# The first large load issued from ScalarE, beside the short first load from SyncE

## The chip, the cores and the metric

One core of one Trainium2 chip, nothing else running on it. The time is that of one execution in device microseconds; a lower number is better.

## The reference

```python
x = np.random.randn(32, 256, 4096).astype(np.float32)
result = np.zeros((32, 256, 256), dtype=np.float32)
for i in range(256):
    result[:, :, i] = np.max(x[:, :, 16 * i : 16 * (i + 1)], axis=-1)
```

Max pooling over windows of 16 floats (64 B): 134 MB are read, 8.4 MB written, and each input is compared once.

## The kernel before

The kernel streams windows through a ring of two slots in SBUF. Each slot has room for 1024 windows and a gap of 152 more (GAP). A load alternates between the start of its slot and a place 152 windows further on. VectorE reduces each load in two parts: first the 872 windows that the next load of this slot will overwrite, then the 152 others. So the next load of a slot waits for the long part only. A short first load (FIRST) uses the gap of slot 0, and its maxima go into `kept` like the others.

```python
CHUNK, GAP, FIRST = 1024, 152, 132
LOADS_A, LOADS_B = 9, 6
last = total - FIRST - (LOADS_A + LOADS_B) * CHUNK          # 892
ring = pool.tile([P, 2 * (CHUNK + GAP) * W], fp32, ...)     # W = 16
# ... pooled(dst, at, n): reduce_max of n windows of the ring on VectorE
for g, loads in enumerate(([FIRST] + [CHUNK] * LOADS_A, [CHUNK] * LOADS_B + [last])):
    ...
    for n in loads:
        if n == FIRST:
            nc.sync.dma_start(out=ring[:, CHUNK * W : (CHUNK + n) * W], in_=xn)
            pooled(dst, CHUNK, n)
        else:
            low = n_loads % 2 * (CHUNK + GAP)
            moved = n_loads // 2 % 2
            at = low + moved * GAP
            nc.sync.dma_start(out=ring[:, at * W : (at + n) * W], in_=xn)
            if n == CHUNK:
                cut = CHUNK - GAP if moved else GAP
                parts = [(0, cut), (cut, n)]
                for u, v in parts if moved else parts[::-1]:
                    pooled(dst[:, u:v], at + u, v - u)
            ...                                             # the last load
            n_loads += 1
# ... one store from ScalarE, two from SyncE
```

In this text S is the short load, L0, L1, L2 are the large ones in order. L0 and L1 fill the two slots at once; L2 goes to slot 0 again and is the first that has to wait. It overwrites S's bytes too.

Of the kernel before, what the change touches and what calls it, by code (L numbers as in the profile page):

```python
# [1 line left out]

# [4 lines left out]


@with_exitstack
def kernel(  # L10
    ctx: ExitStack,
    tc: tile.TileContext,
    x: bass.AP,
    output_size: bass.AP,
    out: bass.AP,
):








    nc = tc.nc
    P = nc.NUM_PARTITIONS
    fp32 = mybir.dt.float32

    B, C, L = x.shape
    O = int(output_size)  # L30
    assert L % O == 0, (L, O)
    W = L // O
    total = B * C * O // P
    assert B * C * O % P == 0

    CHUNK = 1024
    GAP = 152
    FIRST = 132
    LOADS_A, LOADS_B = 9, 6
    last = total - FIRST - (LOADS_A + LOADS_B) * CHUNK  # L40
    assert 0 < last and last * (W + 1) <= CHUNK * W

    pool = ctx.enter_context(tc.tile_pool(name="pool", bufs=1))
    ring = pool.tile([P, 2 * (CHUNK + GAP) * W], fp32, tag="ring", name="ring")
    kept = pool.tile([P, total - last], fp32, tag="kept", name="kept")

    xw = x.flatten_outer_dims().rearrange("r (o w) -> (r o) w", w=W)
    ow = out.flatten_outer_dims().rearrange("r o -> (r o)")

    def pooled(dst, at, n):  # L50

        nc.vector.reduce_max(  # L52
            out=dst,
            in_=ring[:, at * W : (at + n) * W].rearrange("p (n w) -> p n w", w=W),
            axis=mybir.AxisListType.X,
        )

    taken = 0

    def group(n):  # L60

        nonlocal taken
        span = slice(taken * P, (taken + n) * P)
        taken += n
        return (
            xw[span].rearrange("(p n) w -> p (n w)", p=P),
            ow[span].rearrange("(p n) -> p n", p=P),
        )

    stores = []  # L70
    n_loads = 0
    base = 0
    for g, loads in enumerate(
        ([FIRST] + [CHUNK] * LOADS_A, [CHUNK] * LOADS_B + [last])
    ):
        xg, og = group(sum(loads))
        a = 0
        for n in loads:
            xn = xg[:, a * W : (a + n) * W]
            dst = kept[:, base + a : base + a + n] if n != last else None  # L80
            if n == FIRST:

                nc.sync.dma_start(  # L83
                    out=ring[:, CHUNK * W : (CHUNK + n) * W], in_=xn
                )
                pooled(dst, CHUNK, n)
            else:

                low = n_loads % 2 * (CHUNK + GAP)
                moved = n_loads // 2 % 2  # L90
                at = low + moved * GAP
                nc.sync.dma_start(out=ring[:, at * W : (at + n) * W], in_=xn)
                if n == CHUNK:
                    cut = CHUNK - GAP if moved else GAP
                    parts = [(0, cut), (cut, n)]
                    for u, v in parts if moved else parts[::-1]:
                        pooled(dst[:, u:v], at + u, v - u)
                else:
                    end = (at + CHUNK) * W
                    last_kept = ring[:, end - n : end]  # L100
                    pooled(last_kept, at, n)
                n_loads += 1
            a += n
        full = a - last if g else a
        stores.append((og[:, 0:full], kept[:, base : base + full]))
        base += full
    assert taken == total

    nc.scalar.dma_start(out=og[:, full : full + last], in_=last_kept)
    tc.no_sync_barrier()  # L110
    for dst, src in stores:
        nc.sync.dma_start(out=dst, in_=src)


# [1 line left out]
_INS = ['x', 'output_size']  # L116
_OUTS = [((32, 256, 256), 'float32')]

_NUMBERS = {'output_size': 256}


# [26 lines left out]
```

## Time and profile before

| | before |
|---|---|
| time, median | 335.11 us (334.94 to 335.2, 3 runs) |
| span of the profiled execution | 333.4 us |
| VectorE busy | 276.5 us (83%) |
| DMA packets, share of 16 engines | 98.7% + 0.3% |
| L0 lands, L2 issued, L2 lands | 25.14, 39.88, 63.85 us |

### The profile page before, as it was taken

To read this page: it belongs to the slowest core of one execution; us is meant where nothing else is said; L and a number is where in the kernel's file an instruction comes from. 1 tells how busy PE (TensorE), PEld (TensorE's weight loads), DVE (VectorE), ACT (ScalarE), POOL (GpSimd) and SP (SyncE) were. 2 spreads that over 40 slices of the span, in tenths; PEclk is the share of its full clock that TensorE was granted. 3 is DMA by queue.
4 is the path that set the end of the run, shared out by engine and by line. 5 is a ranking of instruction groups with operands and counts; after the bars stand their busy time and mean duration, and the time that the engine had idled before them with its cause. 6 is when DMAs were issued, how large, how long until landed. Compare 5 with 4: busy or idle time off the path is not lost.

```text
span 333.4 us, 113 instructions
## 1 busy us (share of the span) xinstructions
DVE 276.5 (83%) x32; POOL 0.2 (0%) x4
## 2 busy tenths in 40 slices
DVE  2009979797997979799797979979797997979993
POOL 0000000000000000000000000000000000000000
DMA  9898989999898989999898989999898989899997
GB/s 381 377 503 377 495 385 480 401 401 480 377 503 377 503 377 480 401 393 488 377 503 377 503 377 480 401 425 456 377 503 377 503 377 495 385 455 438 397 402 317
DMA packets 2880, 142.61 MB, mean 428 GB/s; under 512 B 320, under 2 KB 320, under 8 KB 448
## 3 DMA queue, kind: packets, MB, share of 16 engines
q1 hardware_dynamic: 2736, 142.15, 98.7%
q10 hardware_dynamic: 144, 0.46, 0.3%
HBM read 134.22 MB, written 8.39 MB: 428 GB/s over the span
## 4 chain that ended last, share of the span: by engine, by line
DMA 58%; DVE 36%; DVEq 5%; issue 0%; SPq 0%
DMA ring<-in_x_dram 58%; DVE kept L52 36%; DVEq L143 5%; SPq L83 0%
## 5 line engine op out<-in xcount | busy, mean ns | idle before, releaser
L52 DVE TENSOR_REDUCE kept<-ring 128x872 f32<-128x13952 f32 (+2 forms) x31 | 261.5, 8477 | 51.8 <-DMA ring<-in_x_dram 51.8
L52 DVE TENSOR_REDUCE ring<-ring 128x892 f32<-128x14272 f32 x1 | 15.0, 15009 | 0.0
L129 POOL MEMSET const-bfloat16-1.0<- 128x1 bf16 x1 | 0.1, 102 | 0.0
L129 POOL MEMSET const-uint8-127<- 128x1 uint8 x1 | 0.1, 102 | 0.0
L129 POOL MEMSET const-float32-1.0<- 128x1 f32 x1 | 0.1, 99 | 0.0
L129 POOL MEMSET const-float32-0.0<- 128x1 f32 x1 | 0.1, 98 | 0.2 <-issue 0.2
## 6 DMA issues: line engine op xcount, KB each, us to landing
ring<-in_x_dram SPq DMA_DIRECT2D x1, 7136.0 KB, 21.5
out_dram<-kept SPq DMA_DIRECT2D x1, 4674.0 KB, 32.2
out_dram<-kept SPq DMA_DIRECT2D x1, 3072.0 KB, 18.0
ring<-in_x_dram SPq DMA_DIRECT2D x1, 1056.0 KB, 5.1
out_dram<-ring ACTq DMA_DIRECT2D x1, 446.0 KB, 4.2
ring<-in_x_dram SPq DMA_DIRECT2D x15, 24.0
```

The lines of the kernel that those rows point to most:

```text
L52: nc.vector.reduce_max(out=dst, in_=ring[:, at * W : (at + n) * W].rearrange("p (n w) -> p n w", w=W), axis=mybir.AxisListType.X,)
L129: nc = _bacc.Bacc("TRN2", target_bir_lowering=False, num_devices=1)
L143: with _tile.TileContext(nc) as tc:
```

## The change

The intent is to start both first loads at once: S from SyncE, L0 from ScalarE. S becomes 128 windows (rows of 8 KB), one load of the first group 1020, and the last 900.

```diff
-    FIRST = 132
+    FIRST = 128
     LOADS_A, LOADS_B = 9, 6
-    last = total - FIRST - (LOADS_A + LOADS_B) * CHUNK
+    LESS = 4
+    group_a = [FIRST] + [CHUNK] * (LOADS_A - 1) + [CHUNK - LESS]
+    last = total - sum(group_a) - LOADS_B * CHUNK
+    group_b = [CHUNK] * LOADS_B + [last]
 ...
-                nc.sync.dma_start(out=ring[:, at * W : (at + n) * W], in_=xn)
-                if n == CHUNK:
+                queue = nc.scalar if n_loads == 0 else nc.sync
+                queue.dma_start(out=ring[:, at * W : (at + n) * W], in_=xn)
+                if n != last:
```

More of the change, by code (lines that the diff above doesn't have):

```diff
@@ L72 @@
     base = 0
-    for g, loads in enumerate(
-        ([FIRST] + [CHUNK] * LOADS_A, [CHUNK] * LOADS_B + [last])
-    ):
+    for g, loads in enumerate((group_a, group_b)):
         xg, og = group(sum(loads))
```

## The prediction

> **What bounds the kernel now.** I began with the page: busy shares by engine, and under them the moved bytes of each DMA queue.
>
> ```profile
> DVE 276.5 (83%) x32; POOL 0.2 (0%) x4
> ...
> q1 hardware_dynamic: 2736, 142.15, 98.7%
> q10 hardware_dynamic: 144, 0.46, 0.3%
> ```
>
> VectorE is busy for 83% of 333.4 us, but the packets of the SyncE queue (q1) fill 98.7% of what 16 DMA engines can give. The ScalarE queue (q10) carries only the last store. So the kernel is a DMA stream: 134.22 MB of loads and 8.39 MB of stores. The second view, busy time and DMA share by stretch, shows that the stream has no holes in the middle, only at its two ends (columns: stretch, length, VectorE busy, GpSimd busy, clock, DMA share, GB/s).
>
> ```profile
> 0.00:5.00 5.00, 0.00 (x0) 0.20 (x4) 1.00 0.83 306
> 25.20:44.50 19.30, 17.25 (x2) 0.00 (x0) 1.00 1.00 435
> 44.50:63.90 19.40, 17.30 (x3) 0.00 (x0) 1.00 1.00 432
> 313.30:328.30 15.00, 14.98 (x2) 0.00 (x0) 1.00 1.01 436
> 328.30:333.40 5.10, 0.00 (x0) 0.00 (x0) 1.00 0.59 244
> ```
>
> A large load is 1024 windows x 64 B x 128 partitions = 8.39 MB; at 433.5 GB/s that is 19.35 us, and the timeline has one large load landing every 19.35 us:
>
> ```profile
> 0.73 0.38 SPq L83 DMA_DIRECT2D ring<-in_x_dram  x1
> 1.16 58.40 SPq L92 DMA_DIRECT2D ring<-in_x_dram  x4
> 5.86 2.35 DVE L52 TENSOR_REDUCE kept<-ring 128x132 f32<-128x2112 f32 x1 [5.86 <-DMA ring<-in_x_dram]
> 25.17 17.28 DVE L52 TENSOR_REDUCE kept<-ring 128x872 f32<-128x13952 f32 x2 [16.96 <-DMA ring<-in_x_dram]
> 44.53 17.28 DVE L52 TENSOR_REDUCE kept<-ring 128x872 f32<-128x13952 f32 x2 [2.08 <-DMA ring<-in_x_dram]
> ```
>
> Call the short load S and the large ones L0, L1, L2. S is reduced at 5.86, L0 at 25.17, L1 at 44.53. The chain of waits alternates, for each pair of loads, a load with the long reduce that frees its slot:
>
> ```profile
> 1.16 23.98 DMA ring<-in_x_dram
> 25.14 0.02 issue
> 25.17 14.70 DVE kept L52
> 39.87 0.02 issue
> 39.88 23.97 DMA ring<-in_x_dram
> ```
>
> The reader should not take the 36% of VectorE in it for a cost. L2 is issued at 39.88 and lands 23.97 later, 4.62 us more than its own 19.35 of transfer: for the most part it sits behind L1. How much of that is slack? The first packets of the kernel come 1.08 us after S is issued (0.73 to 1.81, from the packet records of the trace), so L2 would be ready at about 40.96, and the first engine ends L1 at 43.54. **Slack at the refill: 43.54 - 40.96 = 2.6 us** (an estimate, as the 1.08 is from the start of the kernel). L0 may be reduced up to 2.6 us later and no DMA engine runs dry.
>
> **What the Trainium skill says.** (1) "DMA: Bandwidth & Descriptors", section "Issuing engines are not separate DMA queues": DMAs from different engines run on the same 16 DMA engines and interleave, and issuing from several saves only the sequencer's issue time, "usually small relative to the DMA itself". This trace agrees on the size: an issue is 0.33 to 0.43 us of SyncE time. (2) Same page, "Queues, rings and completion order": each DMA engine goes round-robin over the queues it has work for, packet by packet. What a packet is here decides the case. The records show one packet for each partition's row: 8448 B in 319 ns for S, 65536 B in 2418 ns for a large load, 8 of each per engine, plus a 4 B semaphore packet. The tail says that a packet is not cut into: q10's store was issued at 328.32, yet on each engine its first packet starts some 6 ns after q1's last one and its semaphore packet (330.38 to 330.92 by engine), and q1's last packets take their usual 915 ns. This is no fine sharing; but it doesn't tell turns by packet from turns by whole transfer. (3) "Perfetto Trace Analysis", section "DMA Instruction — HWDGE (DVE, Sync)": an issuing sequencer locks the shared descriptor generator. So the second of two simultaneous issues should come some 0.38 us late; the trace before has no two simultaneous issues to show it. (4) "VectorE: DVE Perf Modes", "The perf-mode tier table (the rule you actually need)": the reduce has only the 1x mode. The trace agrees: 13952 fp32 in 14686 ns, 1.05 ns each.
>
> **The change part by part.**
>
> Removed from SyncE: one issue of 0.43 us. L0's issue moves from 1.16 to about 0.74 on ScalarE, which leaves the start barrier within 0.01 us of SyncE in the records. Worth: nothing by itself, as L0's first packet already follows S's last without a gap (S's packets end by engine at 4.90 to 5.55, L0's begin 6 ns later). The stream starts when the first issue is made, 0.73, and that stays.
>
> Possible gain: the first packets of S take 0.40 to 1.19 us instead of 0.32, so the eight take 3.0 to 3.7 us by engine and not 2.5. A second queue with large packets may hide part of that: at most about 0.5 us, and I expect 0 to 0.3.
>
> Moved: with turns by packet, each engine serves S1 L0-1 S2 L0-2 and so on. S's eighth packet then ends after seven of L0's: about 2.3 + 8 x 0.31 + 7 x 2.414 = 21.7, landed near 22.2 instead of 5.86. Its reduce (128 x 16 elements: 2353 x 128/132 = 2.28 us) ends near 24.5. L0's last packet is at the same place in the stream as before, so L0 lands near 25.1 and is reduced at once. S is needed by nothing earlier: only L2 overwrites its bytes. Cost: 0.
>
> If the generator's lock lets two or three of S's packets by first, S ends earlier, and L1 (next on SyncE's queue) gets a turn before L0's last packet. One such turn delays L0 by 2.42 us, within the slack of 2.6. A second makes 4.84 - 2.6 = 2.2 us of idle DMA.
>
> Sizes: S 132 to 128 windows, one load 1020 in place of 1024, the last 892 to 900. The bytes are the same. The last reduce grows by 15.01 x 8/892 = 0.13 us; the DMA stream (stores) covers that end until 330.4 and the last store needs about 328.45 + 1.08 = 329.5, so most or all of the 0.13 is hidden. The row pitch of group A goes from 598272 to 597760 B, both an odd number of 256 B; I expect no other rate.
>
> Sum: 335.1 + 0 (order) + 0.05 (tail) - 0.1 (start) = 335.1, with one-sided risk above.
>
> **The rivals.**
>
> (A) The two queues share bytes finely instead of packets. After S, L0 and L1 then run at half speed each. L0 ends when S, L0 and an equal part of L1 are through: (64 + 512 + 448) KiB per engine at 27.15 B/ns = 38.6 us after 2.2, landed near 41.2 instead of 25.1. Delay 16.1 - 2.6 slack = 13.5 us of idle DMA, with no way to make it up in a stream that is full afterwards: 348.6 us. For it: some 8 KB instruction packets overlap S's first packets in the records. Against: the uncut packets of the tail. I give it 5%.
>
> (B) An engine stays with q1 as long as q1 has descriptors, or takes a whole transfer of q1 first; or ScalarE's first descriptors come over 2 us late, so that S is through and L0 and L1 alternate. L0 then lands anywhere from 39 to 44 us, and the kernel takes 347 to 352. For it: at the tail the engines took one more q1 packet at 329.47 to 330.01, although the store had been issued 1.15 us or more before. Against: with a descriptor taken one packet ahead, turns look just so. I give 11%, with a part of it at two to five turns lost (337 to 344 us).
>
> (C) The start gap is worth more than I think (two queues fill the engines sooner): 334.3 us. It can't reach 2%, which would be 6.7 us, as all idle DMA time at the start is 1.8 us plus the 0.5 above.
>
> **Range and chances.** The middle case, with up to one lost turn, is 334.6 to 335.4. Two lost turns are 337.3. I take 335.1, a range of 334.4 to 338.0, and put what lies above 2% (341.8), which is (A), (B) and a few lost turns, at 0.16. Faster by 2% is out of reach: 0.01.
>
> **What would show it.** After the change: S's reduce starts near 22 us and not near 6, L0's near 25.2, L1's near 44.5, and the DMA share stays at 1.00 from 25 to 64 us. If S is still reduced before 8 us, L0 must be looked at: at 25 it means turns by whole transfer, at 39 to 44 it is rival A or B, and a stretch of 10 us or more with DMA near 0 follows, between L1's landing and L2's first packet. An L0 near 27.6 is one lost turn, near 30 two. Wrong altogether would be a changed 19.35 us between later landings: then the pitch or sizes matter, not the start.

## The result, and the profile after

The changed kernel takes 337.5 us (median of 6 runs, 336.9 to 337.74) against 334.96 us (6 runs): a ratio of 1.0072, 95% interval 1.0059 to 1.0085. Ratios here are the mean time of one kernel's fast runs over that of the other's of the same rounds, so not quite the ratio of the medians. The profiled execution was the quickest of the six (336.9 us), so the traces differ by less than the medians: 335.1 against 333.4 us.

The DMA issues on the page of the changed kernel (size, then us from issue to landing):

```profile
ring<-in_x_dram SPq DMA_DIRECT2D x1, 1024.0 KB, 24.8
ring<-in_x_dram ACTq DMA_DIRECT2D x1, 25.0
```

S, which landed 5.1 us after its issue before, now takes 24.8, practically as long as L0. The timeline (start, length, what):

```profile
0.73 0.40 ACTq L95 DMA_DIRECT2D ring<-in_x_dram  x1
0.73 0.38 SPq L85 DMA_DIRECT2D ring<-in_x_dram  x1
1.16 58.84 SPq L95 DMA_DIRECT2D ring<-in_x_dram  x3
25.58 36.67 DVE L56 TENSOR_REDUCE kept<-ring 128x128 f32<-128x2048 f32 x5 [25.58 <-DMA ring<-in_x_dram]
65.42 14.69 DVE L56 TENSOR_REDUCE kept<-ring 128x872 f32<-128x13952 f32 x1 [3.17 <-DMA ring<-in_x_dram]
```

Both issues start at 0.73. VectorE does nothing until 25.58; then five reduces follow without a pause, S's first. The chain of waits of the changed kernel:

```profile
0.73 24.82 DMA ring<-in_x_dram
25.55 0.02 issue
25.58 16.89 DVE kept L56 x2
42.47 0.02 issue
42.48 22.91 DMA ring<-in_x_dram
```

Where before one reduce of 14.70 stood between L0's landing and L2's issue, there are now two, 16.89: S's and L0's long one. L2 goes out at 42.48 instead of 39.88, 2.60 us later (0.41 from the landing, 2.19 from the extra reduce), and lands at 65.39 instead of 63.85. The 0.41 belongs to this execution: one of the 16 engines began its first row at 3.00, the others by 2.41, and its semaphore packet for S came at 25.17, the others' by 24.46. In queue_only, s_after_l0 and s_after_l0_same_gap below, S lands at 25.12 to 25.21, practically when L0 landed before, and L2 is late all the same. The stretches of the changed kernel that answer to those of before:

```profile
25.20:44.50 19.30, 18.92 (x3) 0.00 (x0) 1.00 0.97 411
44.50:63.90 19.40, 17.74 (x3) 0.00 (x0) 1.00 0.96 409
```

Before, the DMA share was 1.00 in both, at 435 and 432 GB/s. Here some 24 GB/s are missing over 38.7 us, about 2 us of transfer. From L2 on, loads come every 19.35 us again, so what is lost there stays lost to the end.

The packet records of the trace show both halves of the story. They do not name the engine; rows are put together to one engine where one starts as the other ends. Their times are given on the clock of the views above. In the prediction and in one expectation (extra_64) they were read about 0.07 us late, so the prediction's 1.81 is 1.74, and its 1.08 us from the issue to the first packet is 1.01. Its slack of 2.6 us is unchanged, because 43.54 was late by as much. One of the 16 engines at the start (start in us, length in ns; S are 8 KB rows, L 64 KB rows, sem the 4 B packet that reports the end):

```
changed:  1.76 S 947 | 2.70 L0 2418 | 5.12 S 307 | 5.42 L0 2418 | ... | 21.43 S 309 | 21.74 L0 2418 | 24.15 sem S | 24.16 sem L0 | 24.17 L1
```

The two queues take turns packet by packet. S's eighth data packet is over at 21.74, but its semaphore packet is a packet like others: it waits while L0's eighth row passes. On all 16 engines it follows 2.4 us after S's last data. So S is reported only when L0 is.

And at the refill, over the 16 engines:

```
                L2 issued   L1's semaphore packets   L2's first packets   length of L2's first packets
before            39.88        43.47 to 44.13          43.47 to 44.14        2.42 (one 2.45, one 2.50)
changed           42.48        43.48 to 44.65          43.63 to 45.05        2.63 to 3.43 (one 2.42)
```

Before, each engine goes from L1 to L2 within 0.01 us. After the change 15 of 16 engines wait for L2, or have its first row stretched.

### The profile page after: what moved, and what is told of

Same layout as the page of the kernel before. It is cut to its first block, busy times and chain, and to the rows that moved or that the text cites. A ratio compares the mean times of both kernels' runs of the same rounds, so it can differ in the third digit from the quotient of the medians.

```text
span 335.1 us, 113 instructions
## 1 busy us (share of the span) xinstructions
DVE 276.3 (82%) x32; POOL 0.2 (0%) x4
## 4 chain that ended last, share of the span: by engine, by line
DMA 57%; DVE 36%; DVEq 5%; issue 0%
DMA ring<-in_x_dram 57%; DVE kept L56 36%; DVEq L146 5%
## 5 line engine op out<-in xcount | busy, mean ns | idle before, releaser
L56 DVE TENSOR_REDUCE kept<-ring 128x152 f32<-128x2432 f32 (+3 forms) x31 | 261.2, 8472 | 53.7 <-DMA ring<-in_x_dram 53.7
L56 DVE TENSOR_REDUCE ring<-ring 128x900 f32<-128x14400 f32 x1 | 15.1, 15143 | 0.0
## 6 DMA issues: line engine op xcount, KB each, us to landing
ring<-in_x_dram SPq DMA_DIRECT2D x1, 7200.0 KB, 21.6
ring<-in_x_dram SPq DMA_DIRECT2D x1, 1024.0 KB, 24.8
```

The lines of the kernel that those rows point to most:

```text
L56: nc.vector.reduce_max(out=dst, in_=ring[:, at * W : (at + n) * W].rearrange("p (n w) -> p n w", w=W), axis=mybir.AxisListType.X,)
```

## The experiments

Each kernel was timed in 3 to 5 rounds beside the kernel before, on one chip for each group of four. All results were correct. The theory after reading the traces: the sizes are harmless; S lands with L0, its reduce comes first on VectorE, and L2 is issued too late to reach the engines before L1 is through. The rival: the interleaved start, or a second queue, costs by itself.

**sizes_only**: the changed sizes, all loads from SyncE.

```diff
-                queue = nc.scalar if n_loads == 0 else nc.sync
+                queue = nc.sync
```

> The changed sizes alone (128, 1020, 900), every load from SyncE. My theory: the sizes cost nothing. S lands near 5.8, L0's long reduce starts near 25.1, L2 is issued near 39.9, time 335.0 to 335.3. Rival (sizes or row pitch): 336 or more, and landings further apart than 19.35 us, or a later end by 0.13 us or more for the last reduce.

335.01 us, ratio 1.0001 (0.9989 to 1.0013). S is reduced at 5.46 and L2 issued at 39.52. Sizes, row pitch and the longer last reduce cost nothing measurable.

**queue_only**: the sizes of before, L0 from ScalarE.

```diff
-                nc.sync.dma_start(out=ring[:, at * W : (at + n) * W], in_=xn)
+                queue = nc.scalar if n_loads == 0 else nc.sync
+                queue.dma_start(out=ring[:, at * W : (at + n) * W], in_=xn)
```

> The ScalarE issue alone, with the sizes of before (132, 1024, 892). My theory: all of the loss comes from this part: S lands with L0 near 25.5, S's reduce of 2.35 us comes first, L2 is issued near 42.5, time 337.0 to 337.8. Rival (sizes): 335.1.

337.57 us, ratio 1.0069 (1.0046 to 1.0092); L2 issued at 42.14. The whole loss is in this part. One of the six runs took only 335.3 us: first sign that the kernel sits at an edge.

**s_after_l0** and **s_after_l0_same_gap**: S's reduce written after L0's long one.

```diff
-                pooled(dst, CHUNK, n)
+                first = dst, 2 * CHUNK + GAP, n     # CHUNK in s_after_l0_same_gap; the load goes there
 ...
                     for u, v in parts if moved else parts[::-1]:
                         pooled(dst[:, u:v], at + u, v - u)
+                        if first:
+                            pooled(*first)
+                            first = None
```

> The changed kernel, but S lies in the other slot's gap (where only L3 overwrites it) and VectorE reduces it after L0's long reduce. My theory (the loss is the 2.3 us reduce of S ahead of L0's, which makes the issue of L2 late): L2 is issued near 40.3 and the engines go from L1 to L2 without idling, time 334.8 to 335.3. Rival (the interleaved start itself costs, L0 landing later, or two queues slow the stream): the loss stays at about 2 us, 336.5 to 337.5.

> As the run above, S reduced after L0's long reduce, but S stays where it was, in the gap that L2 overwrites. L0's long reduce starts at once near 25.6, yet L2 has to wait for S's reduce too: 25.6 + 14.7 + 2.3 = 42.6. My theory (only the issue time of L2 counts): 337.0 to 337.8, as the changed kernel. Rival (what counts is when L0's reduce starts): 335.1.

337.51 us (1.0074, 1.0062 to 1.0086) and 337.49 us (1.0063, 1.0043 to 1.0084). Taken at face value the first would refute the theory. But the timeline of s_after_l0 shows that the edit did not take: the scheduler that orders the instructions had put S's reduce in front again.

```profile
25.14 36.66 DVE L56 TENSOR_REDUCE kept<-ring 128x128 f32<-128x2048 f32 x5 [25.14 <-DMA ring<-in_x_dram]
```

A group in this view is named after its first instruction: 128x128, which is S. So these two runs say only that S's place in the ring doesn't matter as long as S is reduced first (L2 issued at 42.05 and 42.14). One of the six runs of s_after_l0_same_gap, not the profiled one, took only 335.19 us, as in queue_only. They were repeated with an ordering barrier.

**l0_first_other_gap** and **l0_first_same_gap**: the same two with the barrier.

```diff
                         if first:
+                            tc.no_sync_barrier()
                             pooled(*first)
```

> What s_after_l0 was meant to be (there the scheduler had put S's reduce first again): with an ordering barrier, VectorE takes L0's long reduce first and S's after it, and S lies where only L3 overwrites it. Theory (late issue of L2 is the whole loss): L2 is issued near 25.2 + 14.7 = 39.9 to 40.3, no engine idles between L1 and L2, 334.8 to 335.3. Rival (the interleaved start or the second queue costs by itself): 336.5 to 337.7.

> The same order on VectorE, but S stays in the gap that L2 overwrites, so L2 waits for S's reduce as well: issue near 25.2 + 14.7 + 2.3 = 42.2. Theory (only the issue of L2 counts): 337.0 to 337.8, like the changed kernel. Rival (the start of L0's reduce counts): about 335.1.

With S in the other slot's gap: 335.41 us, ratio 1.0014 (1.0001 to 1.0027). Its chain of waits has the shape of before, though L0 and S still share the start and land together:

```profile
0.73 24.52 DMA ring<-in_x_dram
...
25.27 14.70 DVE kept L56
...
39.99 23.81 DMA ring<-in_x_dram
```

With S in L2's way: 337.33 us, ratio 1.0077 (1.0065 to 1.0089), although L0's reduce starts at once at 25.19; L2, waiting for S as well, goes out at 42.09:

```profile
25.19 36.66 DVE L56 TENSOR_REDUCE kept<-ring 128x872 f32<-128x13952 f32 x5 [25.19 <-DMA ring<-in_x_dram]
...
25.19 16.89 DVE kept L56 x2
...
42.09 23.78 DMA ring<-in_x_dram
```

The first line is from the timeline (128x872 comes first, which is L0's long reduce), the others from the chain. This pair differs only in the place of S, and so only in L2's issue. What counts is when L2 is issued; the interleaved start and the second queue leave at most 0.4 us (335.41 against 334.98).

**extra_64, extra_96, extra_128, extra_256**: the kernel before, no second queue, with a useless reduce of so many windows ahead of L0's long reduce. Its result is overwritten later.

```diff
+                    if n_loads == 0:
+                        pooled(kept[:, total - last - 128 :], at, 128)
                     for u, v in parts if moved else parts[::-1]:
                         pooled(dst[:, u:v], at + u, v - u)
```

> The kernel before, all loads from SyncE, with a useless extra reduce of 64 of L0's windows (about 1.15 us) ahead of L0's long reduce. L2 is issued near 41.0. Theory, if the slack were the 2.6 us of the prediction: 335.0. As the traces of the changed kernels show L2's first packets on the last engines 2.6 to 3.5 us after its issue, the true slack may be as small as 0.2 to 1 us: then 335.2 to 336.0.

> The kernel before with a useless reduce of 96 windows (about 1.71 us) ahead of L0's long reduce; L2 is issued near 41.5. extra_64 (41.0) lost nothing and extra_128 (41.8 to 42.2) lost either nothing or 2.5 to 3.6 us. Theory (a threshold near 42): 335.0 to 335.2 in all rounds. Rival (a loss that grows from a slack of about 1.2 us): 335.5.

> As extra_64 with 128 windows (about 2.28 us, the size of S's reduce). L2 is issued near 42.2. Theory (a late L2 is enough, without a second queue): 337.0 to 337.7, as the changed kernel. Rival (it takes the second queue): 335.0 to 335.3, for the 2.28 lie within the 2.6 of slack.

> The same with 256 windows (about 4.5 us); L2 is issued near 44.2, after the engines are through with L1. Theory A (beyond the threshold each us of delay costs a us, on top of about 2.5 us for the restart of idle engines): 339.0 to 340.0. Theory B (the loss is only delay less slack, 4.5 - 2.2): 337.2 to 337.6.

| kernel | L2 issued in the profile | median us | single runs |
|---|---|---|---|
| extra_64 | 41.03 | 335.07 | 334.86 to 335.13 |
| extra_96 | 41.31 | 335.10 | 334.96 to 335.29 |
| extra_128 | 41.84 | 336.37 | 335.14, 335.24, 335.28, 337.46, 337.92, 338.58 |
| extra_256 | 44.07 | 337.45 | 337.37 to 337.74 |

Ratios: 1.0002 (0.999 to 1.0014), 1.0002 (0.999 to 1.0015), 1.0049 (1.0017 to 1.008), 1.0074 (1.006 to 1.0088). The delay alone, without ScalarE, brings the loss. And it is a step: nothing up to an issue at 41.31, two groups of runs at 128 windows, with nothing between 335.3 and 337.4. The profiled run of extra_128 is one of the quick ones; its chain has

```profile
24.94 16.89 DVE kept L52 x2
...
41.84 22.04 DMA ring<-in_x_dram
```

so an issue at 41.84 can still be in time, while every profile with an issue from 42.05 on shows the loss. For extra_256 I had expected 339 to 340 if a restart cost 2.5 us on top, and 337.2 to 337.6 if only delay less slack counted; it was the second. There all engines are idle and start L2 0.98 to 1.94 us after the issue, with first rows of 2.42 to 3.58 us. In the runs near the edge some engines get L2 late: in s_after_l0 twelve begin it by 44.09, and four only at 45.12 to 45.45, 3.1 to 3.4 us after its issue at 42.05. So L2 lands at nearly the same time, 66.14 and 66.19, after an issue at 42.05 (s_after_l0) and at 44.07 (extra_256):

```profile
42.05 24.09 DMA ring<-in_x_dram
44.07 22.12 DMA ring<-in_x_dram
```

Why those four engines begin L2 so late was not tried; it stays open.

**halves**: the changed kernel with L0 cut in two loads, so that ScalarE's queue has 16 packets of 32 KB on each engine.

```diff
-                queue.dma_start(out=ring[:, at * W : (at + n) * W], in_=xn)
+                cuts = (0, n // 2, n) if n_loads == 0 else (0, n)
+                for u, v in zip(cuts, cuts[1:]):
+                    queue.dma_start(out=ring[:, (at + u) * W : (at + v) * W],
+                                    in_=xn[:, u * W : v * W])
```

> The changed kernel with L0 cut in two loads of 512 windows on ScalarE's queue, so its packets are 16 of 32 KB per engine. Theory (turns by packet between the queues): S is through after eight of L0's packets, lands near 14, and is reduced at once; then L1 on SyncE's queue takes turns with L0's second half, 64 KB against 32 KB, L0 lands only at 39 to 42 us and the kernel takes 346 to 351 us. Rival (turns by whole transfer, or the queue of ScalarE first): L0 lands near 25 and the time stays at or below 337.5.

353.0 us, ratio 1.0537 (1.0523 to 1.0551), from this timeline:

```profile
15.67 4.88 DVE L56 TENSOR_REDUCE kept<-ring 128x128 f32<-128x2048 f32 x2 [15.67 <-DMA ring<-in_x_dram]
44.88 31.87 DVE L56 TENSOR_REDUCE kept<-ring 128x872 f32<-128x13952 f32 x3 [24.34 <-DMA ring<-in_x_dram]
81.83 14.69 DVE L56 TENSOR_REDUCE kept<-ring 128x872 f32<-128x13952 f32 x1 [5.07 <-DMA ring<-in_x_dram]
```

S lands after eight turns and is reduced at 15.67, where I expected it near 14: its semaphore packet again came one row of L0, here 1.2 us, after its last data. Then L1 takes eight turns beside L0's second half, and L0 lands only at 44.86, 19.7 us late. The turns by packet are thus confirmed, and a little too cautiously sized: I had said 39 to 42 and at most 351. Seven turns of L1 ahead of L0's last row would give that; it took eight (the records show L1's row first in each pair). The changed kernel escapes this only because S and L0 have the same number of packets.

**swapped_l0_first**: as l0_first_other_gap, with L0 on SyncE's queue and S on ScalarE's.

```diff
-                nc.sync.dma_start(              # S
+                nc.scalar.dma_start(
 ...
-                queue = nc.scalar if n_loads == 0 else nc.sync
+                queue = nc.sync
```

> As l0_first_other_gap, but the queues swapped: L0 from SyncE, S from ScalarE. L1 then stands behind L0 in the same queue and can't take a turn before it. Theory: as good as or better than l0_first_other_gap (335.4), 334.8 to 335.3; it beats the kernel before only if the two-queue start is worth something, which I doubt: 334.8 at best.

335.42 us, ratio 1.0012 (1.0 to 1.0025): just above the range expected. Both mended versions end 0.4 us behind the kernel before (all ten runs at 335.19 or more), which is barely clear of the noise, as the intervals begin at 1.0001 and 1.0. The sizes don't explain it, and I did not look further. No version found here beats the kernel before.

## Why the prediction was right or wrong, point by point

- **DMA-bound stream with no holes; sizes and tail free.** Right: sizes_only is at 1.0001. The chance given to a change within 2% (0.83) and the range held.
- **Turns by packet, no fine sharing (rival A), no sticking to one queue (rival B).** Right: seen in the records, and halves shows the price when L1 gets turns.
- **"Its reduce ... ends near 24.5 ... Cost: 0".** This step failed. The data of S was over when predicted (21.6 to 22.8 by engine, against 21.7), but its semaphore packet took a further turn behind L0's last row. S landed at 25.55 and not near 22.2, its reduce came before L0's on VectorE, and L2's issue moved by 2.19 us for it. I had listed the semaphore as a packet and then not given it a turn.
- **"Slack at the refill: 2.6 us".** Too large. It took the time from issue to the first packet of the first engine (1.08 us; rightly 1.01); the last engine counts. By the doses an issue at 41.31 is safe, and in every profile one from 42.05 on is too late, with 41.84 in between: against 39.88 a slack between 1.4 and 2.2 us.
- **The loss as delay less slack.** Wrong near the edge. With 2.60 us of delay and 2.6 of slack the sum would have been 0; the cost is a step of some 2 to 3.6 us. In the traces the engines that run dry start unevenly, and their first rows take up to 3.4 us instead of 2.42.
- **"Two lost turns are 337.3".** The number was nearly the measured one, by accident. No turn was lost: in the trace S and L0 alternate from the first row on all 16 engines, and L1 gets no turn before L0's last row. The range held thanks to a mechanism that did not occur.
- **Gain at the start (0 to 0.3 us, rival C).** Not seen: the mended versions, which have this start without the late L2, are 0.4 us slower than before.
- **Rival A's support, 8 KB instruction packets beside S's first ones.** A misreading, without effect on the sum: in the trace before, the last such packet ends some 8 us before the span begins.
- **Lock of the descriptor generator, second issue 0.38 us late.** Not seen: the two issues overlap from 0.73 and take 0.40 and 0.38 us.

## What to carry to other kernels

In these traces a load that shares the engines with a larger one from another queue ends with it, since both have as many packets, whatever their bytes; count packets, and give the semaphore packet a turn of its own. Before letting a small transfer come late, follow who consumes it in program order: here a harmless 2.3 us reduce moved between a landing and the refill that feeds a full stream. Slack at a refill is to be measured by adding delay in doses, because the cost beyond the edge can be a step and not a slope.

## What the Trainium skill lacked or had wrong

- "DMA: Bandwidth & Descriptors", section "Queues, rings and completion order": it gives a packet as some 9 to 17 descriptors. Here a turn is one row, 8 KB in 309 ns or 64 KB in 2418 ns (the records don't show descriptors). The section says that a semaphore's write lands after the engine's earlier writes, but not that its packet also waits for a turn; it came 2.4 us after the last data of S.
- Same page, "Specifications": about 0.6 us to the first byte for issues from SyncE and ScalarE, without saying from where it counts. The first engine agrees if it counts from the end of the issuing instruction: 0.63 us in the kernel before, 1.01 from its start. What is lacking is the spread over the engines: 16 idle ones began 0.98 to 1.94 us after the start of the issue (extra_256), and near the edge the last one 3.4 us after it (s_after_l0).
- "Perfetto Trace Analysis", section "DMA Instruction — HWDGE (DVE, Sync)": by the lock told there one of two simultaneous issues should take longer. They took 0.40 and 0.38 us, a lone one 0.38.
- No page has what it costs to let the queue run dry for a moment: first rows of up to 3.58 us in place of 2.42, and 2.5 us of 335 lost once.
